# FFN weights in four buffers of their own, one low part by an accumulating DMA, and operands at multiples of 128 bytes

## The chip, the core and the metric

The kernel runs on one core of one Trainium2 chip. The metric is the device time of one execution in microseconds (us). Five engines work side by side, each through its own list of instructions in a fixed order: PE (TensorE, matmuls; its weight loads are listed as PEld), DVE (VectorE), ACT (ScalarE), POOL (GpSimd) and SP (SyncE, which issues most DMAs). A waiting instruction holds up everything behind it on its own engine.

## The reference

A trunk of two layers over 512 tokens of width 1024. Each layer adds half a SwiGLU feed-forward network (FFN) to the residual stream, then a mixer (attention in layer 0, a state space model in layer 1), then half a second FFN, each behind an RMS norm:

```python
def swiglu(h, w_gate, w_up, w_down):
    return (jax.nn.silu(h @ w_gate) * (h @ w_up)) @ w_down
# every layer: x += 0.5*swiglu1(rms(x)); x += mixer(rms(x)); x += 0.5*swiglu2(rms(x))
```

The hidden width of the FFN is 2816, which is 22 tiles of 128 channels. All of it is float32.

## The kernel before

**Phases.** The program is six phases in a row: FFN, attention, FFN, FFN, state space model (ssm), FFN. Here they are called FFN1, attn, FFN2, FFN3, ssm, FFN4. The normed residual stream is held as two operands, `xh` (rounded to the matmul type) and `xl` (the rest). The running sum of squares for the norm is `acc`; one matmul with `onesD` (L135) reduces it, and ACT's L234 and L235 and DVE's L236 to L238 make the reciprocal root `br` from it.

**Products.** `mm3` computes each float32 product as three matmuls: weight high part by `xh` (L120), weight high part by `xl` (L121), weight low part by `xh` (L122). So each weight tile `raw` is split. In `split`, ACT casts `whi<-raw` (L95) and DVE subtracts `wlo<-raw,whi` (L96). In `split_dma`, ACT casts the high part (L107), ACT writes minus the raw tile, rounded, into the low part's buffer (L108), and POOL issues a DMA that adds the raw tile to it (L109), which leaves the rest. Attention and ssm use `split_dma` for their big projections, the FFN uses `split` throughout. All splits of the program share one pool of three `whi` and three `wlo` buffers.

**An FFN.** It runs two halves. Each half has 11 channel tiles of gate and up, then 8 down projections (tile order `DORD`), which read the activations `ah` and `al`. The first one or two channel tiles of an FFN (`direct`) are plain: 16 products of 3 matmuls of 128x512, 48 in all, which run while the norm's last operands are still made. That is 5 tiles in the program. The other 83 use Strassen's scheme: seven half-size products, 84 matmuls of 128x256. Their weights are `raw[:, 0]` (1024 columns: a11 and a12), two sums `sa` and `sb` of 1024 columns (four L1166 instructions, on POOL), and a22 (512 columns). DVE's work for such a tile is four subtractions L96, four combinations L1211, the scaling L1219, the product L1224, and `al<-bs,ah` (L244).

**Order.** The code is in program order; the framework's scheduler makes the fixed list of every engine from it, with its own view of when buffers and inputs are ready. Buffers come from pools that are stacked in memory; a tile waits for the last users of the bytes that it takes.

Of the kernel before, what the change touches and what calls it, by code (L numbers as in the profile page):

```python
# [40 lines left out]
class Trunk:  # L41
    def __init__(self, ctx, tc, aps):
        self.ctx, self.tc, self.nc, self.aps = ctx, tc, tc.nc, aps
        nc = self.nc
        self.cst = ctx.enter_context(tc.tile_pool(name="cst", bufs=1))
        self.wp = ctx.enter_context(tc.tile_pool(name="wp", bufs=3))
# [12 lines left out]
        nc.scalar.preload_act_table_set("natural_log_exp_and_others")  # L59
# [13 lines left out]
    @contextmanager  # L73
    def psum(self, **banks):
# [14 lines left out]
    def split(self, raw, n, lo_engine=None):  # L89

        nc = self.nc
        self.n += 1
        hi = self.wp.tile([P, 8, P], F32R, tag="whi", name=f"whi_{self.n}")
        lo = self.wp.tile([P, 8, P], F32R, tag="wlo", name=f"wlo_{self.n}")
        nc.scalar.copy(out=hi[:, :n], in_=raw)  # L95
        (lo_engine or nc.vector).tensor_tensor(  # L96
            out=lo[:, :n], in0=raw, in1=hi[:, :n].bitcast(F32), op=ALU.subtract
        )
        return hi, lo

    def split_dma(self, raw, n):

        nc = self.nc
        self.n += 1
        hi = self.wp.tile([P, 8, P], F32R, tag="whi", name=f"whi_{self.n}")
        lo = self.wp.tile([P, 8, P], F32R, tag="wlo", name=f"wlo_{self.n}")
# [261 lines left out]
    def values(self, rc):  # L368
# [4 lines left out]
        for c in range(4):  # L373
            raw = self.load(aps["wv"][:, 2 * c : 2 * c + 2], [P, 2, 408])
            self.n += 1
            hi = self.wp.tile([P, 2, 408], F32R, tag="whi", name=f"whi_{self.n}")
            lo = self.wp.tile([P, 2, 408], F32R, tag="wlo", name=f"wlo_{self.n}")
# [748 lines left out]
    def ft(self, shape, tag, bufs=None):  # L1126
        self.n += 1
        return self.F.tile(shape, F32, tag=tag, name=f"{tag}_{self.n}", bufs=bufs)
# [24 lines left out]
    def gu_weights(self, li, fi, f, engine):  # L1153
# [4 lines left out]
        sa, sb = self.ft([P, 8, P], "sa", 1), self.ft([P, 8, P], "sb", 1)  # L1158
# [8 lines left out]
        return a22, [self.split(a, 8) for a in (raw[:, 0], sa, sb)]  # L1167

    def gate_up(self, li, fi, f, ah, al):
# [26 lines left out]
        w = self.split(a22, 4)  # L1196
# [42 lines left out]
    def begin(self, first, ahead=None):  # L1239
# [5 lines left out]
        for i, d in enumerate(DORD):  # L1245
# [4 lines left out]
            sq = self.t512("t1")  # L1250
# [142 lines left out]
```

## Time and profile before

| | |
|---|---|
| time, median of 3 runs | 2236.44 us (2233.39 to 2240.87) |
| the profiled execution: its time | 2238.98 us |
| its span, first to last instruction | 2237.2 us |
| PE busy | 2167.8 us, 97% |
| DVE busy | 1675.6 us, 75% |
| ACT busy | 1154.4 us, 52% |
| POOL busy | 810.3 us, 36% |

The profiled execution has 1.8 us around its span. In the trace FFN1 stands at 0 to 371 us, attn to 694.7, FFN2 to 1044.3, FFN3 to 1390.5, ssm to 1868.7 and FFN4 to the end. One line of the timeline is: start, duration, engine, line of the code, operation, out<-in by the program's names, shapes, and in brackets the idle time before it with what ended it. A matmul's listed duration is longer than the distance to the next one, since matmuls are pipelined; the distance from start to start is what it costs.

### The profile page before, as it was taken

The page shows a single profiled execution, that of the slowest core. Times are in us where ns is not written, and L with a number is a line of the kernel's source. Part 1 is how long each engine was busy: PE and PEld are TensorE (multiplying, and loading weights), DVE is VectorE, ACT ScalarE, POOL GpSimd, SP SyncE. Part 2 cuts the span into 40 slices and gives each one's busy share as a digit, 9 for nine tenths or more (in the row PEclk, how much of TensorE's full clock was granted, in tenths as well). Part 3 has the DMA queues.
Part 4 walks back from the last instruction along what each step waited for, and adds up shares of the span by engine and source line. Part 5 has one row for each costly group of instructions (what it writes and reads, how often), then busy time and mean ns, then how long its engine had stood idle before and what let it go on. Part 6 is the DMA issues. An engine that isn't in the chain of part 4 may idle for free.

```text
span 2237.2 us, 34473 instructions
## 1 busy us (share of the span) xinstructions
PE 2167.8 (97%) x13488; PEld 1935.3 (87%) x13488; DVE 1675.6 (75%) x2430; ACT 1154.4 (52%) x1814; POOL 810.3 (36%) x602
## 2 busy tenths in 40 slices
PE   8999999978999999999999999999999998999998
PEld 5999997867888998998998997788788877998997
DVE  6975984585788975986984984677667668984984
ACT  7533544445566533445542444677667666442543
POOL 1623621432013623622632630244344435622630
PEclk9999999989999999999999999999999999999999
DMA  3222335516302322232322233656565651232322
GB/s 132 95 97 102 107 104 147 133 48 152 76 2 66 114 97 102 96 103 96 112 97 102 95 109 106 172 142 151 118 157 142 160 143 57 104 103 96 114 97 83
DMA packets 48449, 242.04 MB, mean 108 GB/s; under 512 B 6624, under 2 KB 9696, under 8 KB 31136
## 3 DMA queue, kind: packets, MB, share of 16 engines
q1 hardware_dynamic: 36048, 195.28, 25.7%
q0 software_dynamic: 12240, 44.57, 10.5%
q8 instruction: 106, 1.74, 0.3%
q14 instruction: 55, 0.45, 0.1%
HBM read 193.04 MB, written 2.23 MB: 87 GB/s over the span
## 4 chain that ended last, share of the span: by engine, by line
PE 88%; DVE 6%; ACT 2%; DMA 1%; issue 1%; POOL 0%; DVEq 0%; SPq 0%; ACTq 0%; POOLq 0%
PE bm L120 14%; PE bm L122 13%; PE bm L121 13%; PE bs L120 13%; PE bs L122 13%; PE bs L121 13%; DMA wlo<-raw 1%; PE bt L536 1%; DVE xl L244 1%; PE bs L487 1%; DVE wlo L96 1%; PE bo L551 1%; PE bs L482 1%; PE bo L548 1%; PE bs L488 0%
## 5 line engine op out<-in xcount | busy, mean ns | idle before, releaser
L120 PE MATMUL bs<-xh,whi 128*128 128x256 f32 (+1 forms) x2404 | 684.5, 289 | 8.8 <-ACT whi L95 2.9
L121 PE MATMUL bs<-xl,whi 128*128 128x256 f32 (+1 forms) x2404 | 682.0, 286 | 4.1 <-DVE xl L244 4.1
L122 PE MATMUL bs<-xh,wlo 128*128 128x256 f32 (+1 forms) x2404 | 665.5, 287 | 4.5 <-DVE wlo L96 4.5
L95 ACT CAST whi<-raw 128x1024 fp32r<-128x1024 f32 (+3 forms) x312 | 256.8, 826 | 449.4 <-PE bm L121 221.7
L120 PEld LDWEIGHTS bs<-xh,whi 128*128 128x128 f32 x2404 | 452.0, 188 | 25.2 <-issue 9.6
L121 PEld LDWEIGHTS bs<-xl,whi 128*128 128x128 f32 x2404 | 453.4, 189 | 10.8 <-DVE xl L244 5.9
L122 PEld LDWEIGHTS bs<-xh,wlo 128*128 128x128 f32 x2404 | 444.1, 189 | 10.5 <-DVE wlo L96 5.8
L96 DVE TENSOR_TENSOR wlo<-raw,whi 128x1024 fp32r<-128x1024 f32 (+3 forms) x304 | 350.9, 1157 | 111.0 <-ACT whi L95 109.2
L1166 POOL TENSOR_TENSOR sa<-raw 128x512 f32<-128x512 f32 x82 | 111.8, 1364 | 674.2 <-DVE wlo L96 294.5
L121 PE MATMUL bm<-al,whi 128*128 128x512 f32 (+1 forms) x715 | 276.0, 386 | 0.0
L122 PE MATMUL bm<-ah,wlo 128*128 128x512 f32 (+1 forms) x715 | 275.8, 386 | 0.0
L120 PE MATMUL bm<-ah,whi 128*128 128x512 f32 (+1 forms) x715 | 274.8, 386 | 0.0
L109 POOL DMA_DIRECT2D wlo<-raw x85 | 73.6, 866 | 452.6 <-ACT wlo L108 447.2
L1229 DVE SCALAR_TENSOR_TENSOR xT<-bm,xT 128x512 f32<-128x512 f32 (+1 forms) x113 | 77.3, 685 | 165.3 <-PE bm L122 165.3
L122 PE MATMUL bm<-xh,wlo 128*128 128x512 f32 x488 | 195.4, 401 | 4.5 <-DMA wlo<-raw 4.5
L120 PE MATMUL bm<-xh,whi 128*128 128x512 f32 x488 | 195.9, 401 | 1.5 <-DVE xT L1229 0.9
L121 PE MATMUL bm<-xl,whi 128*128 128x512 f32 x488 | 194.5, 399 | 0.0
L1166 POOL TENSOR_TENSOR sa<-sa,raw 128x512 f32<-128x512 f32 x82 | 168.0, 2049 | 5.7
L122 PEld LDWEIGHTS bm<-ah,wlo 128*128 128x128 f32 x715 | 134.3, 188 | 27.1
L121 PEld LDWEIGHTS bm<-al,whi 128*128 128x128 f32 x715 | 134.3, 188 | 26.9
L120 PEld LDWEIGHTS bm<-ah,whi 128*128 128x128 f32 x715 | 134.3, 188 | 26.7
L96 DVE TENSOR_TENSOR wlo<-sb,whi 128x1024 fp32r<-128x1024 f32 x83 | 152.7, 1839 | 1.3 <-ACT whi L95 1.3
(397 smaller groups left out, 4245.2 us busy)
## 6 DMA issues: line engine op xcount, KB each, us to landing
raw<-wgu SPq DMA_DIRECT2D x88, 1024.0 KB
raw<-wdn SPq DMA_DIRECT2D x64, 704.0 KB
wlo<-raw POOLq DMA_DIRECT2D x85, 512.0 KB, 4.7
raw<-m_win SPq DMA_DIRECT2D x24, 1024.0 KB
raw<-m_wout SPq DMA_DIRECT2D x8, 1024.0 KB
raw<-wqk SPq DMA_DIRECT2D x6, 1024.0 KB
raw<-cw SPq DMA_DIRECT2D x4, 1024.0 KB
raw<-wo SPq DMA_DIRECT2D x4, 1024.0 KB
```

The lines of the kernel that those rows point to most:

```text
L95: nc.scalar.copy(out=hi[:, :n], in_=raw)
L96: (lo_engine or nc.vector).tensor_tensor(out=lo[:, :n], in0=raw, in1=hi[:, :n].bitcast(F32), op=ALU.subtract)
L109: nc.gpsimd.dma_start(out=lo[:, :n], in_=raw, accum_op=ALU.add)
L120: nc.tensor.matmul(out, wh, xh, start=start, stop=False)
L121: nc.tensor.matmul(out, wh, xl, start=False, stop=False)
L122: nc.tensor.matmul(out, wl, xh, start=False, stop=stop)
L244: nc.vector.tensor_tensor(out=lo, in0=src, in1=hi.bitcast(F32), op=ALU.subtract)
L482: nc.tensor.matmul(s[j], q_hi, k_hi, start=True, stop=False)
L487: nc.tensor.matmul(s[j], q_hi, k_lo, start=False, stop=False)
L536: nc.tensor.transpose(t[:, at : at + P], p[:, j, k0 : k0 + P], self.idf)
L1166: engine.tensor_tensor(out=out, in0=x, in1=y, op=op)
L1229: self.nc.vector.scalar_tensor_tensor(out=x, in0=b, scalar=scale, in1=x, op0=ALU.mult, op1=ALU.add)
```

## The change

Four things are changed.

1. **Addresses.** A tile of 96 bytes (`edge`) is taken at the right end of memory, so that `xh` and `xl`, which started 96 bytes past a multiple of 128, start at multiples of 128. Every other matmul operand was there already.
2. **Weight buffers.** Every phase opens its own pool: attn and ssm three buffers of each kind as before, an FFN four, and one small pair for a22 (`w4hi`, `w4lo`).
3. **Splits.** The `raw[:, 0]` of each of the 83 Strassen tiles, and both halves of four of the five direct tiles (all but the first of the program), go through `split_dma`: 91 more accumulating DMAs, 91 more ACT instructions, and 91 fewer subtractions on DVE.
4. **Memory for it.** The FFN's `gu` and `e` and its temporary `t1` have one buffer where they had two.

```diff
+        edge = ctx.enter_context(tc.tile_pool(name="edge", bufs=1, side="right"))
+        edge.tile([P, 24], F32, name="edge")
...
+    def weights(self, bufs, small=0):
+        self.n += 1
+        with self.tc.tile_pool(name=f"wp{self.n}", bufs=1, reuse_waits="tile") as self.wp:
+            self.wp_bufs = {8: bufs, 4: small}
+            yield
...
     def split_dma(self, raw, n):
-        hi = self.wp.tile([P, 8, P], F32R, tag="whi", name=f"whi_{self.n}")
-        lo = self.wp.tile([P, 8, P], F32R, tag="wlo", name=f"wlo_{self.n}")
+        hi, lo = self.wtiles()
         nc.scalar.copy(out=hi[:, :n], in_=raw)
         nc.scalar.activation(out=lo[:, :n], in_=raw, func=AF.Copy, scale=-1.0)
         nc.gpsimd.dma_start(out=lo[:, :n], in_=raw, accum_op=ALU.add)
...
-        with tc.tile_pool(name=f"a{li}{fi}", bufs=1, reuse_waits="tile") as ap, tc.tile_pool(
-            name=f"f{li}{fi}", bufs=2, reuse_waits="tile"
-        ) as self.F, self.temps(t1=2, t2=2, s=2), self.psum(s=5, m=2, r=1):
+        with self.weights(4, 1), tc.tile_pool(name=f"a{li}{fi}", bufs=1, reuse_waits="tile") as ap, tc.tile_pool(
+            name=f"f{li}{fi}", bufs=1, reuse_waits="tile"
+        ) as self.F, self.temps(t1=1, t2=2, s=2), self.psum(s=5, m=2, r=1):
...
-        return [self.split(raw[:, m], 8) for m in range(2)]
+        split = self.split if self.direct == 2 and f == 0 else self.split_dma
+        return [split(raw[:, m], 8) for m in range(2)]
...
-        return a22, [self.split(a, 8) for a in (raw[:, 0], sa, sb)]
+        return a22, [self.split_dma(raw[:, 0], 8)] + [self.split(a, 8) for a in (sa, sb)]
...
-        w = self.split(a22, 4)
+        w = self.split(a22, 4, size=4)
```

In the changed listing the three lines of `split_dma` are L121, L122 and L123, `split`'s are L111 and L112, `mm3`'s L134 to L136, and the norm's matmul L149.

**What it moves on the engines.** First DVE in the middle of FFN2's first half, one Strassen tile, before (the number behind an underscore counts tiles):

```order
L96 TENSOR_TENSOR wlo_8283<-raw_8274,whi_8282 128x1024
L1211 TENSOR_TENSOR gu_8262<-gu_8262,bs_8172 128x256
L244 TENSOR_TENSOR al_7188<-bs_8047,ah_7187 128x512
L1211 TENSOR_TENSOR gu_8262<-gu_8262,bs_8170 128x2x256
L96 TENSOR_TENSOR wlo_8287<-sa_8276,whi_8286 128x1024
L1211 TENSOR_TENSOR gu_8262<-gu_8262,bs_8173 128x512
L96 TENSOR_TENSOR wlo_8291<-sb_8277,whi_8290 128x1024
L1219 TENSOR_TENSOR gu_8262<-gu_8262,br_7268 128x1024
L96 TENSOR_TENSOR wlo_8371<-raw_8274,whi_8370 128x512
L1224 TENSOR_TENSOR bs_8171<-gu_8262,bs_8171 128x512
L1211 TENSOR_TENSOR gu_8386<-e_8387,bs_8295 128x2x256
```

And DVE in the second half of FFN2, one Strassen tile, after:

```order
L112 TENSOR_TENSOR wlo_9692<-sa_9680,whi_9691 128x1024
L258 TENSOR_TENSOR al_7222<-bs_9450,ah_7221 128x512
L1228 TENSOR_TENSOR gu_9666<-e_9667,bs_9575 128x2x256
L112 TENSOR_TENSOR wlo_9696<-sb_9681,whi_9695 128x1024
L1228 TENSOR_TENSOR gu_9666<-gu_9666,bs_9576 128x256
L1228 TENSOR_TENSOR gu_9666<-gu_9666,bs_9575 128x2x256
L1236 TENSOR_TENSOR gu_9666<-gu_9666,br_7304 128x1024
L112 TENSOR_TENSOR w4lo_9776<-raw_9678,w4hi_9775 128x512
L1241 TENSOR_TENSOR bs_9575<-gu_9666,bs_9575 128x512
```

Eleven instructions became ten: the subtraction `wlo<-raw` of 1024 columns, which stood between the first two combinations, is gone.

Next PE at the border from attn to FFN2, before: `bm<-qh` and `bm<-ql` are the last output projection, `bs<-xh` and `bs<-xl` the direct tile:

```order
3912 L120 MATMUL bm_7151<-qh,whi_7125 128x512
3913 L121 MATMUL bm_7151<-ql,whi_7125 128x512
3914 L122 MATMUL bm_7151<-qh,wlo_7126 128x512
3915 L120 MATMUL bs_7199<-xh_6946,whi_7191 128x512
3916 L121 MATMUL bs_7199<-xl_6947,whi_7191 128x512
3917 L122 MATMUL bs_7199<-xh_6946,wlo_7192 128x512
3918 L120 MATMUL bs_7200<-xh_6946,whi_7195 128x512
```

The same border on PE, after:

```order
3912 L134 MATMUL bm_7181<-qh,whi_7155 128x512
3913 L135 MATMUL bm_7181<-ql,whi_7155 128x512
3914 L136 MATMUL bm_7181<-qh,wlo_7156 128x512
3915 L149 MATMUL bm_7302<-acc_7004,onesD 128x512
3916 L134 MATMUL bs_7235<-xh_6976,whi_7225 128x512
3917 L135 MATMUL bs_7235<-xl_6977,whi_7225 128x512
3918 L134 MATMUL bs_7236<-xh_6976,whi_7230 128x512
3919 L135 MATMUL bs_7236<-xl_6977,whi_7230 128x512
3920 L136 MATMUL bs_7235<-xh_6976,wlo_7226 128x512
3921 L134 MATMUL bs_7235<-xh_6976,whi_7225 128x512
```

The norm's matmul, 41 places behind the direct tile's first one before (row 3956), now stands ahead of it, and four matmuls on high parts stand ahead of the first one on a low part. At the border from ssm to FFN4 the rows read the same, with the norm's matmul at row 10790 and the direct tile from 10791.

Last ACT at the same border, before, where the casts of the direct tile's two weights stand amid the norm's squares and casts:

```order
512 L243 CAST xh_6946<-s_7028 128x2x256
513 L95 CAST whi_7191<-raw_7189 128x1024
514 L188 ACTIVATE s_7049<-xT,gains 128x512
515 L219 ACTIVATE t_998_7051<-xT 128x512
516 L243 CAST xh_6946<-s_7049 128x512
517 L95 CAST whi_7195<-raw_7189 128x1024
```

And ACT there, after:

```order
556 L257 CAST xh_6976<-s_7195 128x512
557 L257 CAST xh_6976<-t_1031_7294 128x512
558 L248 ACTIVATE t_1036_7306<-bm_7302,epsc 128x512
559 L121 CAST whi_7225<-raw_7223 128x1024
560 L122 ACTIVATE wlo_7226<-raw_7223 128x1024
561 L121 CAST whi_7230<-raw_7223 128x1024
562 L122 ACTIVATE wlo_7231<-raw_7223 128x1024
```

The two casts moved from row 513 and 517, 26 and 22 places ahead of the norm's L234 (row 539), to places behind its counterpart L248, each followed by the write of the low part's buffer.

## Rows read from the trace of the kernel before

**Rows 1.** The page: busy time, share of the span, instructions of each engine.

```profile
PE 2167.8 (97%) x13488; PEld 1935.3 (87%) x13488; DVE 1675.6 (75%) x2430; ACT 1154.4 (52%) x1814; POOL 810.3 (36%) x602
```

**Rows 2.** Stretches: length, busy time (instructions) by engine in the header's order, clock.

```profile
core 0: us, PE busy (x) PEld busy (x) DVE busy (x) ACT busy (x) POOL busy (x), PEclk, DMA share, GB/s
198.80:311.30 112.50, 112.11 (x925) 111.14 (x924) 107.81 (x118) 54.56 (x75) 62.54 (x40) 1.00 0.29 98
...
2053.40:2165.20 111.80, 111.64 (x926) 111.09 (x925) 106.57 (x118) 54.67 (x75) 63.65 (x40) 1.00 0.29 99
694.70:711.30 16.60, 14.92 (x66) 11.20 (x65) 16.57 (x27) 10.00 (x17) 2.65 (x2) 1.00 0.18 63
1868.70:1892.70 24.00, 18.41 (x73) 13.47 (x73) 23.93 (x32) 13.94 (x24) 10.73 (x7) 0.86 0.13 44
1873.30:1880.00 6.70, 5.21 (x13) 3.54 (x12) 6.70 (x9) 4.28 (x8) 4.95 (x5) 0.50 0.37 147
```

**Rows 3.** Timeline at the end of a Strassen tile in FFN2.

```profile
930.20 2.17 DVE L96 TENSOR_TENSOR wlo<-raw,whi 128x1024 fp32r<-128x1024 f32 x1
...
931.41 0.28 PE L122 MATMUL bs<-xh,wlo 128*128 128x256 f32 x1
...
932.49 0.28 PE L122 MATMUL bs<-xh,wlo 128*128 128x256 f32 x1
...
932.82 0.19 PEld L120 LDWEIGHTS bs<-xh,whi 128*128 128x128 f32 x1 [0.26 <-issue]
```

**Rows 4.** Timeline of PE: last down projection of FFN2, then FFN3's direct tile.

```profile
1039.63 0.39 PE L120 MATMUL bm<-ah,whi 128*128 128x512 f32 x1
...
1044.16 0.39 PE L122 MATMUL bm<-ah,wlo 128*128 128x512 f32 x1
1044.39 0.40 PE L120 MATMUL bs<-xh,whi 128*128 128x512 f32 x1
...
1050.01 0.39 PE L120 MATMUL bs<-xh,whi 128*128 128x512 f32 x1
```

**Rows 5.** The page: the accumulating DMAs, POOL's time and us to landing.

```profile
L109 POOL DMA_DIRECT2D wlo<-raw x85 | 73.6, 866 | 452.6 <-ACT wlo L108 447.2
...
wlo<-raw POOLq DMA_DIRECT2D x85, 512.0 KB, 4.7
```

**Rows 6.** Timeline, attn to FFN2: PE, ACT and DVE.

```profile
694.50 0.39 PE L122 MATMUL bm<-qh,wlo 128*128 128x512 f32 x1
694.73 0.40 PE L120 MATMUL bs<-xh,whi 128*128 128x512 f32 x1
...
694.71 1.04 ACT L95 CAST whi<-raw 128x1024 fp32r<-128x1024 f32 x1
...
708.50 0.69 ACT L234 ACTIVATE t<-bm,epsc 128x512 f32<-128x512 f32 x1
...
692.24 2.31 DVE L96 TENSOR_TENSOR wlo<-raw,whi 128x1024 fp32r<-128x1024 f32 x1
...
701.83 1.22 DVE L96 TENSOR_TENSOR wlo<-raw,whi 128x1024 fp32r<-128x1024 f32 x1
```

**Rows 7.** Timeline, ssm to FFN4: PE, ACT and DVE.

```profile
1868.54 0.39 PE L122 MATMUL bm<-yh,wlo 128*128 128x512 f32 x1
...
1888.73 0.66 ACT L234 ACTIVATE t<-bm,epsc 128x512 f32<-128x512 f32 x1
...
1869.92 2.28 DVE L96 TENSOR_TENSOR wlo<-raw,whi 128x1024 fp32r<-128x1024 f32 x1
...
1879.94 2.32 DVE L96 TENSOR_TENSOR wlo<-raw,whi 128x1024 fp32r<-128x1024 f32 x1
```

**Rows 8.** Timeline, FFN3 to ssm: PE and ACT.

```profile
1393.88 0.79 PE L120 MATMUL bm<-xh,t 128*32 128x512 f32 x1
...
1392.82 0.39 ACT L243 CAST t<-raw 128x256 fp32r<-128x256 f32 x1
...
1397.33 0.30 ACT L694 CAST idrm<-idf 128x128 fp32r<-128x128 f32 x1 [1.91 <-DMA idf<-ident]
```

More of the change, by code (lines that the diff above doesn't have):

```diff
@@ L73, in psum, with wtiles @@
     @contextmanager
+    def weights(self, bufs, small=0):
[3 more added lines that the diff above has]
+            yield
+    def wtiles(self, size=8):
+        self.n += 1
+        tag = f"w{size}" if size < 8 else "w"
+        return [
+            self.wp.tile([P, size, P], F32R, tag=tag + p, name=f"{tag}{p}_{self.n}", bufs=self.wp_bufs[size])
+            for p in ("hi", "lo")
+        ]
+    @contextmanager
     def psum(self, **banks):
@@ L87, in row, with split @@
         return self.one.tile([P, T], F32, tag=tag, name=f"{tag}_{self.n}")
-    def split(self, raw, n, lo_engine=None):
+    def split(self, raw, n, lo_engine=None, size=8):
         nc = self.nc
-        self.n += 1
-        hi = self.wp.tile([P, 8, P], F32R, tag="whi", name=f"whi_{self.n}")
-        lo = self.wp.tile([P, 8, P], F32R, tag="wlo", name=f"wlo_{self.n}")
+        hi, lo = self.wtiles(size)
         nc.scalar.copy(out=hi[:, :n], in_=raw)
@@ L103, in split_dma @@
         nc = self.nc
-        self.n += 1
-        hi = self.wp.tile([P, 8, P], F32R, tag="whi", name=f"whi_{self.n}")
-        lo = self.wp.tile([P, 8, P], F32R, tag="wlo", name=f"wlo_{self.n}")
+        hi, lo = self.wtiles()
         nc.scalar.copy(out=hi[:, :n], in_=raw)
@@ L251, in attn @@
         with ExitStack() as ctx:
+            ctx.enter_context(self.weights(3))
             ctx.enter_context(self.temps(t1=2, t2=2, s=2))
@@ L374, in values @@
             raw = self.load(aps["wv"][:, 2 * c : 2 * c + 2], [P, 2, 408])
-            self.n += 1
-            hi = self.wp.tile([P, 2, 408], F32R, tag="whi", name=f"whi_{self.n}")
-            lo = self.wp.tile([P, 2, 408], F32R, tag="wlo", name=f"wlo_{self.n}")
+            hi, lo = (
+                w.rearrange("p a b -> p (a b)")[:, 0:816].rearrange("p (a b) -> p a b", a=2) for w in self.wtiles()
+            )
             nc.scalar.copy(out=hi, in_=raw)
@@ L674, in ssm @@
         with ExitStack() as ctx:
+            ctx.enter_context(self.weights(3))
             ctx.enter_context(self.temps(t1=3, t2=3, s=2))
@@ L1124, in ffn, with ft @@
                     self.last(d, w, ah, al)
-    def ft(self, shape, tag, bufs=None):
+    def ft(self, shape, tag):
         self.n += 1
-        return self.F.tile(shape, F32, tag=tag, name=f"{tag}_{self.n}", bufs=bufs)
+        return self.F.tile(shape, F32, tag=tag, name=f"{tag}_{self.n}")
     def gu_direct_weights(self, li, fi, f):
         raw = self.load(self.aps["wgu"][li, fi, f], [P, 2, 8, P])
-        return [self.split(raw[:, m], 8) for m in range(2)]
+        split = self.split if self.direct == 2 and f == 0 else self.split_dma
+        return [split(raw[:, m], 8) for m in range(2)]
     def gate_up_direct(self, li, fi, f, ah, al):
@@ L1157, in gu_weights @@
         a11, a12, a21, a22 = raw[:, 0, 0:4], raw[:, 0, 4:8], raw[:, 1, 0:4], raw[:, 1, 4:8]
-        sa, sb = self.ft([P, 8, P], "sa", 1), self.ft([P, 8, P], "sb", 1)
+        sa, sb = self.ft([P, 8, P], "sa"), self.ft([P, 8, P], "sb")
         s1, s2, s3, s4 = sa[:, 0:4], sa[:, 4:8], sb[:, 0:4], sb[:, 4:8]
@@ L1248, in begin @@
             self.norm_piece(d, False, late=True)
-            sq = self.t512("t1")
+            sq = self.t512("t1" if i % 3 == 0 else "t2")
             nc.scalar.activation(out=sq, in_=x, func=AF.Square)
```

1 line of the change is left out of this document (removed).

## The prediction

> **What bounds the kernel now.** The page's busy line comes first: PE is busy for 97% of the span, so little is to be had except from the distance between matmuls and from PE's few idle places [rows 1]. I looked for both.
>
> A Strassen stage is 11 tiles of 84 matmuls. Within a tile the distance from start to start is (932.49 - 931.41) / 9 = 0.120 us [rows 3], so 11 tiles need 924 x 0.120 = 110.9 us. Of the four stages with 11 such tiles the first took 112.50 and the last 111.80 [rows 2]. DVE was busy for 107 of these 112 us, at 9.8 us a tile, while PE's floor is 10.08. The place is the tile's end: DVE subtracts `wlo<-raw` for 2.17 us, the combination that frees PSUM for the next tile stands behind it, and the next tile's first weight load comes 0.26 us late [rows 3]. So DVE, nearly full and in a bad order, costs PE some 0.12 us a tile.
>
> The second place is the operands. In the down projection, on `ah` and `al`, twenty matmuls of 128x512 took 1044.16 - 1039.63 = 4.53 us, 0.2265 each; in the direct tile, on `xh` and `xl`, twenty-four took 1050.01 - 1044.39 = 5.62, 0.234 each, with no idle time in either [rows 4].
>
> The third is the borders between phases. Before, PE goes from the last output projection straight into the next direct tile (694.50 to 694.73) [rows 6], and works through it while DVE finishes the norm. It loses time there, but the norm is hidden under the 11 us of direct work.
>
> **The change part by part.**
>
> *DVE relieved, four buffers.* 83 tiles lose the 2.17 us subtraction. DVE then has about 7.7 us of work in a tile of 10.08. The stall of 1.6 us in the first such stage and 0.9 in the last [rows 2] is (1.6 + 0.9) / 22 = 0.114 a tile, and 83 x 0.12 = 10 us go. What takes its place: ACT gains a write of 1.04 us [rows 6], from 54.6 / 11 = 5.0 us a tile to 6.0; POOL gains 0.87 us [rows 5], from 5.7 to 6.6. Both stay below 10.08. The low part lands 4.7 us after its issue [rows 5]; with four buffers its cast stands a tile ahead, which covers 1 + 1 + 4.7. If that cover failed, PE would wait at each tile. I take -10 us, bounds -13 and 0.
>
> *Alignment.* It concerns the 128x512 matmuls on `xh` and `xl`: 1,464 in the input projections of attn and ssm, and 240 in the direct tiles. If the address is the cause of 0.234 against 0.2265, 1,704 x 0.0075 = 13 us go; if it is not, none. Apart from their start the two kinds of matmul are alike in shape and weights, which speaks for it; the stages differ in what runs beside them, so I take 6 ns, that is 0.228, and -10 us, bounds -13 and 0. The 6,972 matmuls of 128x256 on `xh` hang on a weight load of 0.19 us each as well [rows 3], and I give them nothing. The Trainium skill speaks against this part: "TensorE: Matmul & The Clock Gate", in "Wait — 56ns, not 53.3ns?", has the distance as columns over 2.4 GHz plus about 2.5 ns, without a term for the address, which is 0.216 us here. The trace does not agree, since both distances lie above it and differ at one shape; by that rule the part would give nothing and the sum would be 10 us higher.
>
> *The border from attn to FFN2.* The order puts the direct tile's casts behind the norm's L234 on ACT, and the norm's matmul ahead of the tile on PE. PE therefore has nothing from 694.73 on. The L234 of before started at 708.50; two DVE subtractions ahead of it, 2.31 + 1.22, are gone [rows 6], so 705.0. Then 0.6 of L234 in the pipelined row, the cast 1.04, the low part's write 1.04, and the landing 4.7: 712.3. PE has four matmuls on high parts to do by then; the other 44 take 44 x 0.228 = 10.0, so the tile ends at 722.3. Before, PE had by 711.30 done 66 matmuls [rows 2], the 48, the norm's and some 16 small ones worth 1.9 us: the same point was 709.4. The cost is 12.9 us. The clock comes on top: after waits at the border from ssm the granted clock was 0.50 for 6.7 us in which 13 matmuls ran [rows 2], at 1.2 in place of 2.4 GHz, which cost about 13 x 0.2 = 2.6; part of that falls into the wait, so 2. Together +15, bounds +6 (the norm done soon after the last projection) and +17.
>
> *From ssm to FFN4.* The same order. L234 at 1888.73, less 2.28 + 2.32 of subtractions [rows 7]: 1884.1. Plus 0.6, 1.04, 1.04 and 4.7: 1891.5; plus 10.0: 1901.5. Before, 73 matmuls by 1892.70 [rows 2] leave some 23 small ones, 2.8 us: 1889.9. So 11.6, and 2 for the clock: +13.5, bounds +4 and +17.
>
> *From FFN2 to FFN3.* Here the norm is not ahead of the tile. But the new pool starts at the bytes of the phase's last weights, so the first cast waits for the last down matmuls, which end at about 1044.4 [rows 4]. Before, such a cast had its buffer in time, and PE went on without a gap. Cast and write give 1046.5, landing 1051.2, 44 x 0.228 the end at 1061.2, less 0.5 of small products done meanwhile, against 1044.39 + 48 x 0.234 = 1055.6: +5, bounds +3 and +7.
>
> *From FFN3 to ssm.* The small cast `t<-raw`, on which PE's first projection hangs, ran at 1392.82; it now stands behind the cast of `idf`, which waited for its DMA until 1397.33, and behind one more small cast. With 0.3 + 0.3 + 0.4 the matmul can start at 1398.4 against 1393.88 [rows 8]. +4.5, bounds +2 and +6.
>
> *FFN1's start and the border to attn.* ACT gets two writes, DVE loses two subtractions of 1.2 to 2.3 us; the prices are alike. I take 0, bounds -4 and +4.
>
> Sum: -10 - 10 + 15 + 13.5 + 5 + 4.5 = +18. The profiled execution, 2238.98, would become 2257; it stands 2.5 above the median 2236.44, so on the median 2254. I take 2253, since the bounds of the two large borders reach further down than up.
>
> **The rivals.**
>
> *Alignment does nothing.* The two distances are then a property of the stage. +28: 2264.
>
> *The borders are hidden after all.* If DVE's backlog is the whole reason why the norm ended at 708.50 and 1888.73, relief of DVE brings it near the end of the output projection, and both large borders fall to their lower bounds: -18.5, hence 2235. It decides from L234 below 699 and 1875. For it: DVE was busy for 16.57 of 16.60 and 23.93 of 24.00 us there [rows 2]. Against it: of that, the subtractions removed are only 3.5 and 4.6.
>
> *Alignment pays on the small matmuls too*, the case that ends faster. The place is every Strassen tile. If 128x256 on aligned `xh` costs 4 ns less, 6,972 x 0.004 = 28 us go, and the time is 2225. It decides from 2.6 ns, where the sum is zero. For it: half of 0.2265 is 0.113. Against it: the weight load of 0.19 us in each [rows 3], which no address of `xh` shortens.
>
> *The low part lands late in every tile.* POOL carries the four sums and the DMA's issue in one row, and DVE slows POOL. If PE waits 0.3 us a tile, 83 x 0.3 = 25 replace the 10 gained: 2288. The rule that stands behind it is in the Trainium skill, "SBUF — State Buffer", section "SBUF: two separate sides": descriptors of DMAs issued by POOL are written by GpSimd, which an operation of DVE can lock out of a shared port. The trace agrees so far as `wlo<-raw` on DVE took 2.17 us beside POOL's sums and 1.22 elsewhere [rows 3, 6]; whether landing suffers, no row shows. For the change: a tile's lead of 10 us against 6.7.
>
> **How the numbers follow.** A measurement of this kernel tells a difference from about 0.3%, 6.7 us, on. Forecast 0.53, 2244 to 2263. Alignment nothing 0.10, 2264. Late landing 0.08, 2288. Borders hidden 0.16, of which 0.12 within 0.3% and 0.04 faster. Small matmuls 0.13, of which 0.11 faster and 0.02 within. Faster: 0.15; same: 0.14; slower: 0.53 + 0.10 + 0.08 = 0.71. The range takes the bounds of the forecast and the borders and leaves out the late landing and the better part of the small matmuls: 2230 to 2270.
>
> **What would show it.** In the trace after: PE idle for some 10 us or more behind the last projection of attn and of ssm, ended by ACT's cast and then by the DMA of `wlo`; a Strassen stage of 11 tiles at 111 us with DVE at about 85 us busy; 128x512 matmuls on `xh` at 0.227 to 0.228. The forecast is wrong if PE's idle time at the two large borders is below 6 us, or if a Strassen stage is above 113.

## The result, and the profile after

| | before | after |
|---|---|---|
| time, median (lowest to highest) | 2235.06 us (2233.39 to 2240.87) | 2331.34 us (2327.24 to 2335.27) |
| span of the profiled execution | 2237.2 us | 2333.5 us |
| PE busy | 2167.8 us, 97% | 2181.6 us, 93% |
| DVE busy | 1675.6 us, 75% | 1578.4 us, 68% |
| ACT busy | 1154.4 us, 52% | 1235.9 us, 53% |
| POOL busy | 810.3 us, 36% | 806.7 us, 35% |

The changed kernel takes 1.0416 times the time of before, with a 95% interval from 1.0399 to 1.0434. The direction was forecast, the size was not: +96 us against +17. The page of the kernel after, its busy line, queue 0 (all accumulating DMAs), the chain that ended last, three groups of instructions, and the landing of the low parts:

```profile
PE 2181.6 (93%) x13488; PEld 1951.4 (84%) x13488; DVE 1578.4 (68%) x2339; ACT 1235.9 (53%) x1905; POOL 806.7 (35%) x693
...
q0 software_dynamic: 25344, 92.29, 21.3%
...
PE 61%; DMA 11%; DVE 11%; issue 9%; POOL 4%; ACT 4%; SPq 0%; DVEq 0%; POOLq 0%; ACTq 0%
...
L136 PE MATMUL bs<-xh,wlo 128*128 128x256 f32 (+1 forms) x2072 | 603.4, 293 | 40.0 <-DMA wlo<-raw 39.6
L134 PE MATMUL bs<-xh,whi 128*128 128x256 f32 (+1 forms) x2072 | 606.1, 294 | 28.2 <-ACT whi L121 11.0
...
L123 POOL DMA_DIRECT2D wlo<-raw x176 | 152.7, 868 | 562.0 <-ACT wlo L122 548.5
...
wlo<-raw POOLq DMA_DIRECT2D x176, 512.0 KB, 5.1
```

DVE lost 97 us with the 91 subtractions that left it, 1.07 each [rows 1], and PE got no shorter for it. PE still has 13488 matmuls, but it now waits, and the largest named reason is new: 39.6 us ahead of a matmul on a low part (L136), ended by the DMA of `wlo`. There are 176 of these DMAs in place of 85 [rows 5]. A tenth of the chain is now DMA.

**Where the 96 us are.** In both traces the stages can be laid side by side, from the start of one matmul to the start of another: the two halves of each FFN up to their first down projection, and the borders from the last projection of one phase to the end of the next direct tile. Small FFN matmuls that ran before that end (15 and 22 at the large borders before, 4 at FFN3 after) are counted in the first half, at 0.12 us each.

| stretch | before | after | difference |
|---|---|---|---|
| second halves, 11 Strassen tiles each: FFN1, FFN2, FFN3, FFN4 | 112.5, 112.5, 112.5, 111.8 | 120.2, 120.0, 115.6, 119.4 | +26.0 |
| first halves, behind the direct tiles (FFN1 from the start): FFN1, FFN2, FFN3, FFN4 | 139.0, 102.9, 103.1, 103.8 | 145.7, 107.2, 114.3, 107.4 | +6.7 +4.3 +11.2 +3.6 |
| border attn to FFN2 | 14.8 | 32.1 | +17.3 |
| border ssm to FFN4 | 21.4 | 35.9 | +14.5 |
| border FFN2 to FFN3 | 11.2 | 18.7 | +7.5 |
| border FFN3 to ssm (first projection after the last down) | 3.4 | 7.0 | +3.6 |
| rest of ssm, attn | 474.7, 322.3 | 479.1, 319.6 | +4.4 -2.6 |
| 8 down projections, each half | 59.6 | 59.6 | 0 |

The rows add up to 96.5 us, and the end of FFN4 is 0.3 shorter; the spans differ by 96.3. More than half, 51.8, comes from the Strassen halves, for which a gain of 10 was forecast.

**A Strassen stage.** Stretches of the kernel after: the second halves of FFN1 and FFN2, and the two large borders from the end of the last projection to the end of the direct tile (length, busy time by engine, then clock, DMA share, GB/s):

```profile
core 0: us, PE busy (x) PEld busy (x) DVE busy (x) ACT busy (x) POOL busy (x), PEclk, DMA share, GB/s
205.70:325.70 120.00, 114.50 (x925) 113.87 (x924) 94.42 (x108) 63.50 (x85) 58.38 (x48) 0.97 0.50 136
905.50:1025.50 120.00, 114.59 (x926) 113.98 (x925) 94.84 (x108) 63.42 (x85) 58.49 (x48) 0.97 0.49 133
706.50:738.60 32.10, 17.56 (x52) 11.88 (x52) 17.80 (x28) 16.76 (x24) 8.23 (x9) 0.68 0.44 115
1939.50:1975.40 35.90, 16.54 (x52) 11.13 (x51) 23.42 (x29) 20.02 (x30) 15.28 (x12) 0.67 0.39 103
```

Against 112.50 with DVE at 107.81 and a clock of 1.00 in the same stage [rows 2], DVE is 13 us freer, and the stage is 7.5 us longer. No engine is full. PE is idle for 5.4 us and runs part of the rest at the lower level, 1.2 in place of 2.4 GHz, so that the stretch's mean clock is 0.97. The waits in FFN2's second half name the two ends of the trouble (us in total, times, longest):

```profile
POOL sa L1183 <- DMA raw<-wgu: 33.0, 7, 8.7
...
PE bs L136 <- DMA wlo<-raw: 5.4, 3, 2.1
```

And the chain of this stage, one round of it (start, us, what):

```profile
940.70 2.32 DVE w4lo L112
943.09 4.78 DMA raw<-wgu
948.02 1.30 POOL sa L1183
949.38 1.16 issue
950.55 1.75 POOL sa L1183
952.30 7.83 DMA wlo<-raw
960.18 0.48 PE bs L136
960.66 0.21 PE bs L134
960.87 0.21 PE bs L135
961.09 0.21 PE bs L136
```

This is read as follows. `w4lo`, the subtraction for a22, is the last reader of a raw tile. There are two raw tiles, so its end releases the load of the tile after next. The load lands, POOL makes the sums from it, and only behind three of the four sums in POOL's row stands the DMA that completes the low part. It lands 7.8 us later, and PE has been waiting for it. After this wait the matmuls stand 0.21 us apart in place of 0.12. Such a wait comes three times in the stage (at 936, 958 and 992, of 1.5, 2.1 and 1.7 us), that is every second or third tile; the matmuls behind the first of them kept their 0.12.

**The border from attn to FFN2**, timeline after, PE, ACT and POOL:

```profile
706.27 0.39 PE L136 MATMUL bm<-qh,wlo 128*128 128x512 f32 x1
...
714.09 2.08 PE L149 MATMUL bm<-acc,onesD 128*128 128x512 f32 x2 [7.43 <-DVE acc L237]
...
716.94 0.69 ACT L248 ACTIVATE t<-bm,epsc 128x512 f32<-128x512 f32 x1
717.52 1.03 ACT L121 CAST whi<-raw 128x1024 fp32r<-128x1024 f32 x1
718.46 1.06 ACT L122 ACTIVATE wlo<-raw 128x1024 fp32r<-128x1024 f32 x1
...
718.61 0.79 PE L134 MATMUL bs<-xh,whi 128*128 128x512 f32 x1 [2.45 <-ACT whi L121]
...
719.81 0.88 POOL L123 DMA_DIRECT2D wlo<-raw  x1 [11.61 <-ACT wlo L122]
...
725.72 0.79 PE L136 MATMUL bs<-xh,wlo 128*128 128x512 f32 x1 [4.00 <-DMA wlo<-raw]
```

PE has nothing to do from 706.5 on but the norm's matmul, then waits for ACT's cast, and then for the low part. Before, it went on after 0.23 us [rows 6]. At the border from ssm to FFN4 the wait for the norm alone is 12.05 us.

### The profile page after: what moved, and what is told of

It is laid out like the page before. It is cut to its first block, busy times and chain, and to the rows that moved or that the text cites. A ratio compares the mean times of both kernels' runs of the same rounds, so it can differ in the third digit from the quotient of the medians.

```text
span 2333.5 us, 34661 instructions
## 1 busy us (share of the span) xinstructions
PE 2181.6 (93%) x13488; PEld 1951.4 (84%) x13488; DVE 1578.4 (68%) x2339; ACT 1235.9 (53%) x1905; POOL 806.7 (35%) x693
## 4 chain that ended last, share of the span: by engine, by line
PE 61%; DMA 11%; DVE 11%; issue 9%; POOL 4%; ACT 4%; SPq 0%; DVEq 0%; POOLq 0%; ACTq 0%
PE bm L134 12%; PE bm L136 12%; PE bm L135 12%; DMA wlo<-raw 6%; PE bs L136 6%; PE bs L134 5%; PE bs L135 5%; DMA raw<-wgu 5%; POOL sa L1183 3%; DVE gu L1228 2%; DVE w4lo L112 1%; DVE wlo L112 1%; ACT whi L111 1%; PE bt L551 1%; DVE al L258 1%
## 5 line engine op out<-in xcount | busy, mean ns | idle before, releaser
L136 PE MATMUL bs<-xh,wlo 128*128 128x256 f32 (+1 forms) x2072 | 603.4, 293 | 40.0 <-DMA wlo<-raw 39.6
L134 PE MATMUL bs<-xh,whi 128*128 128x256 f32 (+1 forms) x2072 | 606.1, 294 | 28.2 <-ACT whi L121 11.0
L135 PE MATMUL bs<-xl,whi 128*128 128x256 f32 (+1 forms) x2072 | 604.4, 292 | 1.4 <-DVE xl L258 1.4
L136 PEld LDWEIGHTS bs<-xh,wlo 128*128 128x128 f32 x2072 | 402.8, 195 | 52.0 <-DMA wlo<-raw 47.2
L134 PEld LDWEIGHTS bs<-xh,whi 128*128 128x128 f32 x2072 | 405.1, 196 | 43.0 <-ACT whi L121 17.1
L123 POOL DMA_DIRECT2D wlo<-raw x176 | 152.7, 868 | 562.0 <-ACT wlo L122 548.5
L121 ACT CAST whi<-raw 128x1024 fp32r<-128x1024 f32 x176 | 184.6, 1049 | 257.0 <-PE bm L135 108.9
L134 PE MATMUL bm<-ah,whi 128*128 128x512 f32 (+1 forms) x715 | 274.8, 386 | 0.0
L136 PE MATMUL bm<-ah,wlo 128*128 128x512 f32 (+1 forms) x715 | 274.5, 386 | 0.0
L111 ACT CAST whi<-raw 128x640 fp32r<-128x640 f32 (+2 forms) x138 | 110.6, 803 | 272.7 <-PE bm L135 210.1
L134 PE MATMUL bm<-xh,whi 128*128 128x512 f32 x488 | 194.9, 399 | 4.5 <-DVE x L869 1.9
L136 PE MATMUL bm<-xh,wlo 128*128 128x512 f32 x488 | 193.7, 398 | 4.1 <-DMA wlo<-raw 4.1
L112 DVE TENSOR_TENSOR wlo<-sa,whi 128x1024 fp32r<-128x1024 f32 x83 | 124.7, 1503 | 97.1 <-ACT whi L111 97.0
L122 ACT ACTIVATE wlo<-raw 128x1024 fp32r<-128x1024 f32 x176 | 185.5, 1054 | 8.3 <-DMA raw<-wqk 6.7
L112 DVE TENSOR_TENSOR wlo<-raw,whi 128x640 fp32r<-128x640 f32 (+2 forms) x130 | 118.0, 908 | 99.0 <-ACT whi L111 95.8
L1228 DVE TENSOR_TENSOR gu<-gu,bs 128x512 f32<-128x512 f32 (+1 forms) x249 | 148.0, 594 | 25.8 <-PE bs L136 17.5
L136 PEld LDWEIGHTS bm<-ah,wlo 128*128 128x128 f32 x715 | 134.3, 188 | 27.1
```

Source lines behind the costliest of these rows:

```text
L112: (lo_engine or nc.vector).tensor_tensor(out=lo[:, :n], in0=raw, in1=hi[:, :n].bitcast(F32), op=ALU.subtract)
L122: nc.scalar.activation(out=lo[:, :n], in_=raw, func=AF.Copy, scale=-1.0)
L123: nc.gpsimd.dma_start(out=lo[:, :n], in_=raw, accum_op=ALU.add)
L134: nc.tensor.matmul(out, wh, xh, start=start, stop=False)
L135: nc.tensor.matmul(out, wh, xl, start=False, stop=False)
L136: nc.tensor.matmul(out, wl, xh, start=False, stop=stop)
```

## Experiments

Each time is set against the kernel before, run on the same chip; where the text says "after", its ratio of 1.0416 is meant.

### The alignment alone

The kernel before with the tile of 96 bytes, and nothing else:

```diff
+        edge = ctx.enter_context(tc.tile_pool(name="edge", bufs=1, side="right"))
+        edge.tile([P, 24], F32, name="edge")
```

> The kernel before with the 96-byte edge tile alone. If the start address sets the distance of the 128x512 matmuls on xh and xl, it falls from 233.5 to 228 or 229 ns there, 1,704 of them give back about 8.5 us, and the time is 2226 to 2229. If the address does nothing, the time is 2235 within 3 us and the distance stays at 233.

Measured: 2229.83 us against 2237.78, ratio 0.9963 [0.9951, 0.9976], so -8 us, just short of the gain expected. The cause is seen in the distance of matmuls on `xh` and `xl`. Timeline of PE in attn's input projections, before, in e1_align and after:

```profile
386.23 0.39 PE L122 MATMUL bm<-xh,wlo 128*128 128x512 f32 x1
...
393.22 0.40 PE L122 MATMUL bm<-xh,wlo 128*128 128x512 f32 x1
```

```profile
383.68 0.39 PE L122 MATMUL bm<-xh,whi 128*128 128x512 f32 x1
...
387.53 0.39 PE L124 MATMUL bm<-xh,wlo 128*128 128x512 f32 x1
```

```profile
402.03 0.39 PE L136 MATMUL bm<-xh,wlo 128*128 128x512 f32 x1
...
406.11 0.39 PE L136 MATMUL bm<-xh,wlo 128*128 128x512 f32 x1
```

Before, 30 matmuls took 6.99 us, 0.233 each; in e1_align 17 took 3.85 us, 0.2265 each, and after, 18 took 4.08 us, 0.2267 each, which is what those on `ah` take [rows 4]. Over all 128x512 matmuls on `xh` and `xl` the mean distance, waits left out, falls by 5 ns from before to e1_align (0.235 to 0.230 in the projections, 0.234 to 0.229 in the direct tiles); 1,704 times that is 8 us, the whole gain. The 128x256 matmuls of the Strassen tiles stay at a median of 0.120.

### Three ways to leave DMAs out

The low part of `raw[:, 0]` back on DVE, in the kernel after (e2_dve); the direct tiles back on DVE (e5_direct):

```diff
-        return a22, [self.split_dma(raw[:, 0], 8)] + [self.split(a, 8) for a in (sa, sb)]
+        return a22, [self.split(a, 8) for a in (raw[:, 0], sa, sb)]
```

```diff
-        split = self.split if self.direct == 2 and f == 0 else self.split_dma
-        return [split(raw[:, m], 8) for m in range(2)]
+        return [self.split(raw[:, m], 8) for m in range(2)]
```

> The changed kernel with raw[:, 0] of the Strassen tiles split by DVE again; four buffers, pools by phase, alignment and the direct tiles by DMA stay. Theory 1, the accumulating DMA of the Strassen tiles costs what the eight Strassen stages lost (51 us together): stages of 11 tiles fall from 119 or 120 us to 111 to 113, and the time to about 2280. Theory 2, the pools by phase and the new order cost it: the stages stay at 118 to 120 us and the time above 2315.

> The changed kernel with the direct tiles split by DVE again, the Strassen tiles still by DMA. If the landing of the low part is one half of the borders' loss, the three borders into a direct tile get 4 to 7 us shorter each (attn to FFN2 32.0, FFN2 to FFN3 18.7, ssm to FFN4 35.8 us in the changed kernel) and the time is 2310 to 2320. If only the place of the casts counts, it stays within 5 us of 2331. The Strassen stages stay at 115 to 120 us in both.

Measured: e2_dve 2290.49 us, ratio 1.0244 [1.0221, 1.0267]; e5_direct 2315.21 us, ratio 1.0347 [1.0322, 1.0372]. So the DMA in the Strassen tiles costs 1.7% of the time, some 38 us, and that in the direct tiles 0.7%, some 15 (e5_direct rests on two executions, as e4_pools, e6_first and e11_gu2 below do). The stretch of FFN2's second half with its down projections, in e2_dve:

```profile
886.60:1057.40 170.80, 170.80 (x1189) 160.22 (x1188) 140.04 (x172) 80.40 (x117) 66.97 (x42) 1.00 0.28 96
```

It took 172.4 before and 180 after. PE is never idle in it, although DVE makes the subtraction again. So the gain that was forecast for these stages is there without the DMA; the experiments on the buffers, below, show where it comes from.

Half of it by DMA (e9_half): the columns of a11 by DMA, those of a12 by DVE.

```diff
-    def split_dma(self, raw, n):
+    def split_dma(self, raw, n, m=None):
...
+        m = m or n
...
-        nc.scalar.activation(out=lo[:, :n], in_=raw, func=AF.Copy, scale=-1.0)
-        nc.gpsimd.dma_start(out=lo[:, :n], in_=raw, accum_op=ALU.add)
+        nc.scalar.activation(out=lo[:, :m], in_=raw[:, :m], func=AF.Copy, scale=-1.0)
+        nc.gpsimd.dma_start(out=lo[:, :m], in_=raw[:, :m], accum_op=ALU.add)
+        if m < n:
+            nc.vector.tensor_tensor(out=lo[:, m:n], in0=raw[:, m:n], in1=hi[:, m:n].bitcast(F32), op=ALU.subtract)
...
-        return a22, [self.split_dma(raw[:, 0], 8)] + [self.split(a, 8) for a in (sa, sb)]
+        return a22, [self.split_dma(raw[:, 0], 8, 4)] + [self.split(a, 8) for a in (sa, sb)]
```

> The changed kernel, where of a Strassen tile's raw[:, 0] only the first 512 columns (a11) get their low part by ACT and the accumulating DMA, and DVE subtracts the other 512. Theory 3a, the low part misses PE by 1.5 to 2.3 us in every second or third tile because its landing is stretched by the load of the next weights: half the bytes land 2 us or more sooner, the stages of 11 tiles fall from 120 us to 110.9 to 113 and the time to 2280 to 2295. Theory 3b, the load itself is late, and with it every split of the tile: the stages stay above 117 us and the time above 2320.

Measured: 2294.35 us, ratio 1.0253 [1.0238, 1.0269], nearly that of no DMA. A second half with its down projections takes 173.3 to 173.8. Waits in FFN2's second half (895 to 999), and the landings there of ten halves:

```profile
POOL sa L1186 <- DMA raw<-wgu: 27.3, 8, 6.1
...
PE bs L139 <- DMA wlo<-raw: 0.7, 1, 0.7
```

```profile
DMA to landing us min/median/max: 3.3/4.9/6.7
```

The raw tile is still late: POOL waits for it 27.3 us, against 33.0 after. PE waits for a low part once, for 0.7 us, against three times and 5.4, although its first product in a tile (a11) still hangs on the DMA. What is shorter is the end of the chain: the halves land in 4.9 us in the median and 6.7 at most, against 6.0 and 8.3 after (shown below), and ACT's write in front of the issue has half the columns. So the first of the two expectations came true: a landing one to two us shorter takes most of the loss away while the load stays late.

### What makes the low part late

A third raw buffer should let the load start earlier. It has room only with three weight buffers, so the control e3_raw2 has those and two raw buffers, and e3_raw3 has three of each (both open the pool of raw tiles by phase; the line of e3_raw3, shortened at the three dots):

```diff
-        with self.weights(4, 1), tc.tile_pool(...) as ap, tc.tile_pool(
+        with self.weights(3, 1, 3), tc.tile_pool(...) as ap, tc.tile_pool(
```

> The changed kernel with the pool of raw tiles opened by each phase, two buffers as before, and three weight buffers in the FFN: the control for the next run. All theories expect Strassen stages of 11 tiles at 118 to 122 us, as in the changed kernel.

> As the run before, with three raw buffers in the FFN. Theory 1a, a raw buffer is held until the accumulating DMA that reads it has landed, so the load of the tile after next comes too late: with a third buffer the stages of 11 tiles fall to 111 to 113 us, and POOL's waits for the load of wgu (34.6 us in the second stage) vanish. Theory 1b, the low part itself lands too late for PE whatever the loads do (5 to 7 us behind POOL's sums): the stages stay above 117 us.

Measured, one run each: 2342.62 and 2351.99 us. The third raw buffer did not help. The control tells why this is no answer: with three weight buffers the cast of the high part waits for PE to leave its buffer. Waits in e3_raw3, whole program:

```profile
ACT whi L122 <- PE bs L136: 277.1, 72, 7.2
...
PE bs L137 <- DMA wlo<-raw: 43.1, 64, 2.9
```

That wait, 277 us in 72 casts, stands in front of the low part (275 us in 71 casts in e3_raw2), so an earlier raw tile could not come into effect. The pair is inconclusive on the raw buffers and shows something else: with three weight buffers PE waits for a low part 64 times, for 2.9 us at most (26 times after, with four).

The DMA first in POOL's row (e6_first): the four sums are held until the tile's DMA has been issued.

```diff
+        w0 = self.split_dma(raw[:, 0], 8)
...
+            with self.tc.issue_after(self.acc_dma.ins):
```

> The changed kernel with the four sums of a Strassen tile on POOL held behind the issue of that tile's accumulating DMA, which stood behind three of the four. Theory 2a, the low part is late because POOL issues its DMA 4 us after the tile's load has landed: stages of 11 tiles fall from 120 us to 111 to 114 and the time to 2285 to 2300. Theory 2b, the sums on POOL are themselves as late (the load is late, since the raw buffer is given back by a22's subtraction at the end of the tile): the sums move back by 3 us, the stages stay at 118 to 123 us and the time above 2325.

Measured: 2366.64 us, ratio 1.0577 [1.0551, 1.0603], 35 us worse than after. POOL now waits for ACT's write ahead of the sums (18.8 us between 930 and 1050, and 20.3 us for DVE's `w4lo`), and the sums, on which four of the seven products hang, come late instead. Turning the two round does not mend the chain.

Two causes are left: that the raw tile comes late, and that its load, moving beside the accumulating DMA, stretches the landing. In the trace after, a DMA beside which no load moves lands in 4.5 us, one beside 1 MB of loads in some 7 (medians of some 60 and 50 of them). Two runs take the load out of the chain. In both, all Strassen tiles of a stage use a11, a12 and a21 of the stage's first tile, so the weights of the other tiles are left out of the result. In e13_early the load of every tile still runs, and a22's split reads it; e12_noload leaves this load out and splits the first tile's a22 each time.

```diff
-        raw = self.load(self.aps["wgu"][li, fi, f], [P, 2, 8, P])
-        a11, a12, a21, a22 = raw[:, 0, 0:4], raw[:, 0, 4:8], raw[:, 1, 0:4], raw[:, 1, 4:8]
+        if f % HF == (self.direct if f < HF else 0):
+            self.held = self.load(self.aps["wgu"][li, fi, f], [P, 2, 8, P])
+            self.late_raw = self.load(self.aps["wgu"][li, fi, f], [P, 2, 8, P])
+        else:
+            self.nc.sync.dma_start(out=self.late_raw, in_=self.aps["wgu"][li, fi, f])
+        raw = self.held
+        a11, a12, a21, a22 = raw[:, 0, 0:4], raw[:, 0, 4:8], raw[:, 1, 0:4], self.late_raw[:, 1, 4:8]
...
-            (s1, a21, a22, ALU.add),
+            (s1, a21, raw[:, 1, 4:8], ALU.add),
```

e12_noload has `held` alone, without the second load and without the `else`.

> The changed kernel, where the four sums and the accumulating DMA of every Strassen tile read one tile of weights that is loaded at the stage's start and held (so all tiles of a stage use the first one's a11, a12 and a21, and the output is not the reference's). The load of every tile stays: its 1 MB goes to the other buffer, from which only a22's split reads, so it still begins when the subtraction w4lo of the tile before has ended. Theory 'the load's collision stretches the landing': the load still moves beside the accumulating DMA, landings of 5 to 8 us stay, and so do stages of 118 to 120 us; the time stays within 10 us of the changed kernel's, 2320 to 2335. Theory 'the raw tile comes too late, since its buffer is released by w4lo, and the sums ahead of the DMA on POOL wait for it': sums and DMA no longer wait for a load, PE's waits for the low part go, stages of 11 tiles at 111 to 112 us in spite of landings of 5 to 8, and the time falls by 4 x 8 plus the shorter share of the other stages, to 2280 to 2297.

> The changed kernel, where all Strassen tiles of a stage read one tile of weights that is loaded once at the stage's start, so that no load runs beside the accumulating DMAs of the other tiles (the output is not the reference's). Both theories (the load's collision, the load's lateness) expect stages of 11 tiles at 111 us and a time of 2280 to 2297, with landings of 4.5 us. If the stages stay at 118 to 120 us neither is right, and what makes PE wait is the place of the cast and the DMA in ACT's and POOL's rows. Against the run with the load kept this one shows what the collision alone is worth: nothing by the lateness theory, all by the other.

Measured: e13_early 2290.76 us, ratio 1.0242 [1.0222, 1.0262]; e12_noload 2290.21 us, ratio 1.0241 [1.0221, 1.0261]. FFN2's second half in e13_early, and its low parts:

```profile
887.70:998.60 110.90, 110.90 (x925) 110.87 (x924) 92.49 (x106) 63.72 (x84) 56.26 (x48) 1.00 0.57 150
```

```profile
DMA to landing us min/median/max: 4.5/5.5/6.1
```

and the low parts of the same stage after:

```profile
DMA to landing us min/median/max: 4.5/6.0/8.3
```

With the bytes still moving (150 GB/s over a shorter stage, against 133), nothing that the low part hangs on waits for a load, and the stage is back at PE's floor. Taking the load away altogether (landings 4.5 to 4.9) gives no more. So without the wait for the raw tile the DMA's 40 us in the Strassen tiles are gone.

This does not make the late tile the only cause. As the accumulating DMA no longer follows the landing of the load, only about a quarter of a MB of it moved beside most of them in e13_early, not the 1 MB beside five of ten after, so the landings became shorter as well; what one of 8 us beside an early tile would do is not shown. And e9_half lost most of its waits with the tile still late. What the runs show together is a chain of load, sums and landing that is up to about 2 us too long: the late tile and the stretched landing are both in it, and to shorten it at either end was enough.

### The buffers without the DMA

The kernel before with the pools per phase, three weight buffers and the small pair for a22, single `gu` and `e` buffers, and neither the DMA nor the alignment (e4_pools), and the same with two `gu` buffers (e11_gu2):

```diff
-        self.wp = ctx.enter_context(tc.tile_pool(name="wp", bufs=3))
+        with self.weights(3, 1), tc.tile_pool(name=f"a{li}{fi}", bufs=1, reuse_waits="tile") as ap, tc.tile_pool(
+            name=f"f{li}{fi}", bufs=1, reuse_waits="tile"
+        ) as self.F, self.temps(t1=1, t2=2, s=2), self.psum(s=5, m=2, r=1):
...
-        w = self.split(a22, 4)
+        w = self.split(a22, 4, size=4)
```

```diff
-        t = self.ft([P, 7, 256], "gu")
+        t = self.ft([P, 7, 256], "gu", 2)
```

> The kernel before with weight pools opened by each phase (three buffers, and in the FFN the small pair for a22) and the FFN's single buffers; no edge tile, every FFN split on DVE. If the pools alone move the direct tile's casts behind the norm, PE is idle for 9 to 13 us behind the last projection of attn and 13 to 18 behind that of ssm, where it was not idle before, and the time is 2250 to 2265. If the idle time comes from the DMA's landing, the borders cost what they did before and the time is 2225 to 2240.

> The run with pools by phase and no DMA in the FFN (2274 us), with two buffers of gu. If the single gu is what makes FFN3's second tile wait for the norm (7.8 us idle there), that idle time goes and the time is 2264 to 2268. If the new order does it, it stays at 2274.

Measured: 2273.78 us, ratio 1.0162 [1.0137, 1.0187], above the range expected, and 2266.68 us, 1.0131 [1.0112, 1.0149]. In these kernels the second halves take 110.9 to 111.7 us without any relief of DVE. The borders are the largest loss: 25.6 us from attn to FFN2 and 33.0 from ssm to FFN4 in e4_pools, 10.8 and 11.7 more than before. So of the +17.3 and +14.5 after, the pools bring 63 and 81%; the rest is the low parts by DMA in the direct tile, since e5_direct, without these, has 25.0 and 32.5.

The single `gu` shows at FFN3's second tile. Timeline after, DVE and PE:

```profile
1116.24 1.64 DVE L252 SCALAR_TENSOR_TENSOR br<-t,t 128x512 f32<-128x512 f32 x1
1117.91 1.22 DVE L1236 TENSOR_TENSOR gu<-gu,br 128x1024 f32<-128x1024 f32 x1
...
1120.53 0.69 DVE L1228 TENSOR_TENSOR gu<-e,bs 128x512 f32<-128x512 f32 x1
1121.14 0.69 DVE L258 TENSOR_TENSOR al<-bs,ah 128x512 fp32r<-128x512 f32 x1
...
1121.89 0.58 PE L134 MATMUL bs<-xh,whi 128*128 128x256 f32 x1 [6.75 <-DVE al L258]
```

The first combination of the Strassen tile (L1228) must wait until the direct tile's `gu` is scaled by `br`, the norm's result, and used. PE stands for 6.75 us meanwhile, released right behind it in DVE's row (L258). In e4_pools that wait is 7.6, with two `gu` buffers 2.3 and 1.5 more behind it; FFN3's first half, here from the end of the direct tile with nothing moved, takes 111.8 and 107.4, against 102.9 before and 113.6 after. So the second `gu` buffer gives back about half of what is lost there.

### Small pair for a22, shared weight pool kept

The aligned kernel of the first experiment with a22's pair in the FFN's own pool, `e` single (e8_a22), and with `e` double and `t1` single (e10_best):

```diff
-        w = self.split(a22, 4)
+        w = self.split(a22, 4, pool=self.F)
...
-        e1 = self.ft([P, 256], "e")
+        e1 = self.ft([P, 256], "e", 1)
```

> The kernel before with the edge tile and a small pair of buffers for a22 in the FFN's pool (e with one buffer to make room); one weight pool of three for the program, all FFN splits on DVE. If the rotation of four splits through three buffers was what put the subtractions in a bad order, the 1 to 1.5 us that each Strassen stage loses go and the time is 2216 to 2222. If DVE's load is the reason, the stages stay at 112.5 and the time at 2228 to 2231.

> The kernel before with the edge tile, the small pair for a22 in the FFN's pool, two buffers of e again and one of t1 in the FFN. If the stages keep 110.8 us and the rest is as in the kernel with the edge tile alone, 2216 to 2222. If the new order again costs the borders and ssm what the stages gain, 2228 to 2242.

Measured: 2241.39 us, ratio 1.0019 [1.001, 1.0028], slower than either case expected, and 2233.5 us, 0.9976 [0.9966, 0.9986]. The second halves are at 110.9, PE's floor, in both. That is 1.6 to 1.8 us less in each of four stages than with the alignment alone. The whole is not better, since as much and more is lost elsewhere: FFN3's first half from its first small matmul takes 106.1 us in both against 102.6, and ssm, from FFN3's last down projection on, 482.1 and 477.7 against 475.2. The lowest ratio of all runs is that of the alignment alone, which beats both the kernel before and the one after.

## Why the prediction was wrong

**Strassen tiles, forecast -10, measured +51.8: the step that failed.** It was "The low part lands 4.7 us after its issue [rows 5]; with four buffers its cast stands a tile ahead, which covers 1 + 1 + 4.7." Two things in it are wrong. The cast stands a tile ahead only if the raw tile is there a tile ahead, and that hangs on a buffer that the step did not look at: the two raw tiles, released by `w4lo` at the end of DVE's row for the tile before. The sequence was not counted from its start: 4.8 us of load, some 4 of sums and issue, then the landing, 7.8, are 17 us between the release and PE. And the landing of 4.7 was read from a median over ssm and attention; in FFN2's second half it was 4.5 to 8.3 with a median of 6.0. The chain missed PE's need by up to about 2 us: with the raw tile held (e13_early) or the landing shortened (e9_half) most of the loss goes, so neither error alone had to cost this.

The forecast's reason for a gain was right in part. The stages can run at 110.9 us, as e8_a22 and e13_early do. But it is not the lighter DVE that brings this: in e8_a22 DVE still makes every subtraction. Taking a22 out of the rotation of the weight buffers is enough. And DVE's relief in the kernel after was 1.2 us a tile in place of 2.17: its 107.81 us fell to 94.42 in FFN1's second half, not to some 85.

**The rival "the low part lands late in every tile"** had the right place and direction. Its price of 0.3 us a tile was too low: 51.8 / 83 is 0.62 (with FFN3's wait for `gu` in it), and in FFN2's second half (120.0 - 110.9) / 11 is 0.83, of which 5.4 / 11 = 0.49 is waiting; the rest is mostly the lower clock after two of the waits. It got 0.08, since its own mechanism, DVE slowing POOL and its issue, was weak: the issue takes 868 ns after and 866 before [rows 5]. The rule named beside it, from the Trainium skill, "SBUF — State Buffer", section "SBUF: two separate sides", that DVE can lock GpSimd out while descriptors are written, is not needed to explain any of it, and no run here singles it out.

**Alignment, forecast -10, measured -8.** The step held, and the rival "alignment does nothing" falls. So does the one in which the small matmuls gain. The formula in the Trainium skill, "TensorE: Matmul & The Clock Gate", section "Wait — 56ns, not 53.3ns?", has no term for the address; the trace does not agree, as one shape ran at 0.233 and at 0.2267 depending on where its operand began.

**The borders, forecast +15, +13.5, +5 and +4.5, measured +17.3, +14.5, +7.5 and +3.6.** This part held, though the first and the third end just above their upper bounds of 17 and 7. These 43 us against 38 are the share of the slowdown that was foreseen; the Strassen halves went the other way than forecast. L248, the step's pivot, came 10.4 us after attn's last projection against 10.3 forecast, and 16.6 after ssm's against 15.3. The excess at the first is in the direct tile: 20.0 us from its first matmul (718.61) to its end (738.6), against the 15.7 that the forecast has from the end of the cast on. Its first low part landed in 5.9 us and not 4.7, and the 44 matmuls behind it took 12.9 us and not 10.0, since the first 13 or so ran at 1.2 GHz, 0.43 apart; for the clock the forecast had 2. From FFN2 to FFN3 the tile's matmuls also stood 0.43 apart (1092.9 to 1096.7), and there the sum had no term for the clock. The border from FFN3 to ssm has the right size for a wrong reason:

```profile
1458.73 2.05 PE L149 MATMUL bs<-acc,onesD 128*128 128x512 f32 x2 [5.10 <-DVE acc L237]
...
1460.24 0.96 PE L134 MATMUL bm<-xh,t 128*32 128x512 f32 x1
```

PE waits for the norm's sum first, and then for the small cast. On ACT the cast of `idf` did not wait for its DMA; the small cast `t<-raw` stood behind four casts and writes of the projections' weights, about 1 us each, and ran at 1459.79.

**What the sum did not have.** The single `gu` in FFN3, where one wait of 6.75 us stands; it was on the list of the change and got no term. And the rest of ssm: it is 4.4 us longer, where alignment alone made ssm 2.9 shorter, so some 7 us are lost there. PE's idle time in ssm rose from 478.1 - 465.6 = 12.5 to 486.0 - 464.6 = 21.4 us, 5.1 of it the border's wait. The order of the scan differs in every kernel with new pools (ssm, from FFN3's last down projection on, took 475.9 to 490.5 in them, 478.1 before), and what in it costs the time is not settled. Nor is the 6.7 in FFN1's first half taken apart, where the change also puts two of three squares at the program's start into `t2`, which its list does not name.

**The clock** follows the waits as the forecast had it for the borders, 0.67 and 0.68 in these stretches. That short waits inside a stage can also bring the lower level was not in it: in FFN2's second half those of 2.1 and 1.7 us were followed by matmuls 0.21 us apart, the one of 1.5 was not, and neither was one of 2.5 in FFN4's second half.

## What to carry to other kernels

When work is moved from an engine to a DMA, count the whole chain that leads to its issue, from the event that frees the input buffer through everything that stands ahead in the issuing engine's row, and not only the landing. A chain that is too long can be shortened at either end. A buffer count is a lead only for the buffer that is scarcest: here four weight buffers gave no lead of a tile while two raw tiles, released late, paced the chain. And do a change's parts one by one: of those tried here, the smallest, 96 bytes of padding, has the lowest time.

## What the runs showed of the hardware

- A 128x512 matmul whose moving operand starts 96 bytes past a multiple of 128 stood 0.233 us from the next, an aligned one 0.2267; at 128x256 the median was 0.120 either way.
- An accumulating DMA of 512 KB landed in 4.5 us by itself, in some 7 beside 1 MB of weight loads, and in FFN2's second half in up to 8.3; one of 256 KB in 3.3 by itself and up to 6.7 in that stage.
- In FFN2's second half waits of PE of 2.1 and 1.7 us inside a busy stage were each followed by matmuls 0.21 in place of 0.12 us apart, at 1.2 GHz, and one of 1.5 us was not. Of the 9.1 us by which the stage stood above its floor 5.4 were idle time, and the rest, 3.7, was mostly these slower matmuls.
